# A hybrid decoder trunk: the first layer's input read features-first, ten idle products ahead, and the last sum and its transfers divided anew

## The chip, the cores and the metric

The kernel runs on one core of a Trainium2 chip. Its engines are TensorE (PE: products; PEld: the loading of their stationary operand, which overlaps), VectorE (DVE), ScalarE (ACT), GpSimd (POOL, unused here but for four constants) and SyncE (SP), which issues most of the transfers. Each engine works off its own queue in order. The metric is the device time of one execution in microseconds, taken as the median of several runs.

## What is computed

Two layers of a decoder trunk over 256 tokens of 2048 features, all float32. Each layer normalises x, multiplies it by one wide matrix, runs three mixers on parts of the result, gates and merges them, and adds the projection back to x. At the end there is one more normalisation.

```python
def rms_norm(x, w):
    y = xf * lax.rsqrt(jnp.mean(xf * xf, axis=-1, keepdims=True) + EPS)
    return (y * w.astype(jnp.float32)).astype(x.dtype)

def hybrid_layer(x, norm_w, w_in, ...):
    h = rms_norm(x, norm_w)
    proj = h @ w_in                      # 2048 x 18064
    (qa, ka, va, za, qi, ki, wi, ub, zb, qc, kc, vc, zc, gates) = jnp.split(...)
    ...                                  # sparse attention, conformer conv, stick-breaking attention
    merged = g[:, :, 0] * y_a + g[:, :, 1] * y_b + g[:, :, 2] * y_c
    return x + merged @ w_out

def reference(x, ...):
    for i in range(DEPTH):               # 2
        x = hybrid_layer(x, ...)
    return rms_norm(x, final_norm_w)
```

## The kernel before, in words

Every float32 product is made from two halves. A matrix of weights arrives in `raw` by a transfer from SP (`load_unit`, 512 KB: two chunks of 128 inputs by 512 outputs, or four by 256), ScalarE casts it to the rounded type (`wh`, line 204), VectorE subtracts to get the low part (`wl`, line 208), and TensorE adds up wh × x_high, wh × x_low and wl × x_high (line 218 records all of these). `raw` has four buffers, `wh` and `wl` three each, so ScalarE's cast of one unit waits until TensorE has done with the unit three before. Transfers are asked for one after the other on SP's queue, each held behind the transfer kept in `first` at the beginning.

What matters here is the beginning of a layer and the end of the last one.

The beginning. Two column blocks of the wide matrix (512 columns of `O_UG`, then 512 of `O_UA`) are multiplied by x before x is normalised, in `chunk_first`: 16 chunks of 128 features in eight units of two chunks, 24 products of 256 tokens a unit. In layer 0 the first unit is loaded as two halves of 256 KB. The normalisation's factor is worked out meanwhile, and the results are scaled by it afterwards (`rb`, a row broadcast over the partitions). For this, x is needed with features on the partitions. x lies tokens-first in memory, so in layer 0 `start_0` has each quarter of x turned by TensorE (`x_turn`, line 373, eight transposes for four chunks), multiplied by the norm weights on the way out of PSUM by VectorE (line 383, in the first unit ScalarE too, line 382), rounded by ScalarE (line 385) and its low part taken by VectorE (line 386). ScalarE squares the tokens-first x (line 366) and sums along the row with its accumulator; `rsqrt_mean` makes the factor, `diag_cols` a diagonal matrix of it (line 307), and `spread` multiplies ones by that matrix (line 422) between the two chunks to get `rb` (line 423). While the second chunk runs, `follow` scales x by rb (`scale_x`, line 411), rounds it (line 412) and takes low parts (line 417), two chunks of features a unit. From then on the layer uses these `hx`.

In both chunks of layer 0's start the order on VectorE is the program's, and in the first chunk that of ScalarE and TensorE too (`manual_schedule`); elsewhere a scheduler orders by priority.

The constants (identity, ones, norm weights, masks, rotary tables, convolution weights) are one DRAM array; the first 288 columns come first of all (line 63), the other 1696 after the ninth load (line 199).

The end. In layer 1 the output projection is done in blocks of 512, 512, 512, 256 and 256 columns. The last 256 columns are done for 128 tokens at a time (48 products each). After each of these two, the block is added to x (line 889), squared and summed by ScalarE (line 894) into the fifth of five partial sums, multiplied by the final norm weight (line 895); then VectorE adds the five sums (line 391), `rsqrt_mean` makes the factor (lines 291 to 296), and four quarters of 512 columns are scaled, two by VectorE (line 936) and two by ScalarE (line 934), each followed by its transfer on SP's queue (line 937).

Of the kernel before, what the change touches and what calls it, by code (L numbers as in the profile page):

```python
# [8 lines left out]
F32 = mybir.dt.float32  # L9
# [33 lines left out]
C_ID, C_ONE, C_NW, C_CB, C_SM, C_UP, C_MEAN, C_COS, C_SIN, C_PR = (  # L43
    0, 128, 256, 288, 544, 672, 800, 928, 1184, 1440)
# [4 lines left out]
def trunk(ctx: ExitStack, tc: tile.TileContext, x, w_in, w_a, w_b, w_c, w_out,  # L49
# [12 lines left out]
    with tc.high_priority(offset=URGENT):  # L62
        first = [nc.sync.dma_start(cst[:, :C_CB], consts[:, :C_CB])]

    xcs = []

    def load_x(j, cols=((0, 512),)):
        for a, b in cols:
            if a == 0:
                xcs.append(tp.tile([P, NT, 512], F32, tag="t4", bufs=4, name=f"x0_{j}"))  # L70
            with tc.high_priority(offset=URGENT), tc.issue_after(first[0].ins):
                first[0] = nc.sync.dma_start(xcs[j][:, :, a:b], xin[:, :, j * 512 + a:j * 512 + b])

    load_x(0, ((0, 256),))
# [106 lines left out]
    def load_unit(w, k0, kn, segs, dst=None):  # L181
# [5 lines left out]
        with tc.high_priority():  # L187
            o = 0
            for c0, c in segs:
                with tc.issue_after(first[0].ins):  # L190
                    dma = nc.sync.dma_start(
                        raw[:, :, o:o + c],
                        w[k0 * P:(k0 + kn) * P, c0:c0 + c].rearrange("(k p) c -> p k c", p=P))
                o += c
            if count[0] <= 5:
                first[0] = dma
            if count[0] == 9:
                with tc.issue_after(dma.ins):
                    first[0] = nc.sync.dma_start(cst[:, C_CB:], consts[:, C_CB:])
# [53 lines left out]
    def chunk_first(act, units):  # L253
        acc = acc_tile()
        for k0 in range(0, KD, 2):
            ks, between = units(k0)
            for n, (j, i) in enumerate(((0, 0), (0, 1), (1, 0))):
                if n == 1 and between:
                    between()
                for k, w_ in ks:  # L260
                    for f in range(4):
                        mm = mult(acc[:, f // 2, (f % 2) * S:(f % 2) * S + S], w_[j][:, f * P:(f + 1) * P],
                                  part(act, i, k)[:, 0, :], k == 0 and n == 0 and f % 2 == 0,
                                  k == KD - 1 and n == 2)
            background(mm)
# [33 lines left out]
    def warm_sqrt():  # L299
        d = small(1, 2)  # L300
# [75 lines left out]
    def x_parts(ps, xn, k, nw, n=2, first=False):  # L376
        xT, ux = xn
        xs = xT[k // KC][:, k % KC:k % KC + n, :]
        i = k % 4
        if first:  # L380
            for j in range(n):
                nc.scalar.activation(hi(ux, k + j), ps[:, i + j:i + j + 1, :], AF.Copy, scale=nw[:, k + j:k + j + 1])  # L382
        nc.vector.tensor_mul(xs, ps[:, i:i + n, :], nw[:, k:k + n].unsqueeze(2).to_broadcast([P, n, S]))
# [11 lines left out]
    warm_sqrt()  # L395
    xn = (big(), parts(KD))
    ssq = small(8).rearrange("p (t j) -> p t j", t=NT)
    tail = None
    for layer in range(DEPTH):
        w = w_in[layer]  # L400
        nw = cst[:, C_NW + layer * KD:C_NW + (layer + 1) * KD]
# [5 lines left out]
        with tc.manual_schedule(engines={nc.vector.engine}), ExitStack() as order:  # L407
            def scale_x(i):
                k = i * 2
                xs = xT[k // KC][:, k % KC:k % KC + 2, :]  # L410
                nc.vector.tensor_mul(xs, xs, heads(rb, 2))
# [15 lines left out]
            def follow(k0):  # L427
                u = k0 // 2
                if u == 0:
                    spread(state["dg"])  # L430
                else:
# [12 lines left out]
                return advance_units(k0)  # L444
# [28 lines left out]
            def step(ps, k):  # L473
                high(loaded[0])
                rest = x_parts(ps, xn, k, nw)
                low(loaded[0])
                ready.append(loaded.pop(0))
                rest()
# [509 lines left out]
```

## Time and profile before

| | us |
|---|---|
| median of 3 runs | 2072.56 (2072.18 to 2073.11) |
| the profiled execution | 2072.41 |
| its span, first to last instruction | 2070.6 |
| TensorE busy | 2056.9 |
| VectorE busy | 1490.4 |
| ScalarE busy | 1067.4 |
| DMA, mean rate over the span | 190 GB/s |

The page of the profile gives busy times over the span; the chain of waits follows the work that ended last back to its releasers; a timeline lists instructions as start, duration, engine, line, operation, output and inputs, shape and count, and in brackets how long the engine had been idle and what ended that. Rows of a timeline are merged where an engine repeats itself. A windows row gives a stretch, its length, the busy time and number of instructions of PE, PEld, DVE, ACT and POOL, the granted clock, the share of the DMA engines' time and their rate. All times are from the start of the span.

### The profile page before, as it was taken

The page shows a single profiled execution, that of the slowest core. Times are in us where ns is not written, and L with a number is a line of the kernel's source. Part 1 is how long each engine was busy: PE and PEld are TensorE (multiplying, and loading weights), DVE is VectorE, ACT ScalarE, POOL GpSimd, SP SyncE. Part 2 cuts the span into 40 slices and gives each one's busy share as a digit, 9 for nine tenths or more (in the row PEclk, how much of TensorE's full clock was granted, in tenths as well). Part 3 has the DMA queues.
Part 4 walks back from the last instruction along what each step waited for, and adds up shares of the span by engine and source line. Part 5 has one row for each costly group of instructions (what it writes and reads, how often), then busy time and mean ns, then how long its engine had stood idle before and what let it go on. Part 6 is the DMA issues. An engine that isn't in the chain of part 4 may idle for free.

```text
span 2070.6 us, 28574 instructions
## 1 busy us (share of the span) xinstructions
PE 2056.9 (99%) x11056; PEld 1793.6 (87%) x11056; DVE 1490.4 (72%) x2037; ACT 1067.4 (52%) x1309; POOL 0.2 (0%) x4
## 2 busy tenths in 40 slices
PE   9999999999999999999999999999999999999998
PEld 8899888888888888888899998888888888888887
DVE  7678998688776856555576799976887757565555
ACT  6465555466444544444454655554664445444443
POOL 0000000000000000000000000000000000000000
PEclk9999999999999999999999999999999999999999
DMA  7677575665666666666666774756656667666664
GB/s 247 194 220 214 145 204 157 182 179 165 180 190 189 217 209 192 187 190 194 206 191 194 224 204 145 203 152 187 182 162 183 190 194 223 193 192 190 206 196 145
DMA packets 290984, 394.27 MB, mean 190 GB/s; under 512 B 16544, under 2 KB 181536, under 8 KB 290720
## 3 DMA queue, kind: packets, MB, share of 16 engines
q1 hardware_dynamic: 289760, 390.35, 63.6%
q8 instruction: 86, 1.41, 0.3%
q10 hardware_dynamic: 1088, 2.10, 0.3%
q14 instruction: 50, 0.41, 0.1%
HBM read 388.20 MB, written 4.19 MB: 190 GB/s over the span
## 4 chain that ended last, share of the span: by engine, by line
PE 99%; DMA 0%; DVE 0%; ACT 0%; issue 0%; ACTq 0%; SPq 0%
PE acc L218 95%; PE mm L653 1%; PE mm L684 1%; PE mm L373 0%; PE mm L709 0%; PE mm L824 0%; PE mm L772 0%; PE mm L736 0%; PE mm L701 0%; PE mm L758 0%; PE mm L624 0%; PE mm L739 0%; PE mm L774 0%; DMA x<-in_x_dram 0%; PE mm L760 0%; PE mm L763 0%
## 5 line engine op out<-in xcount | busy, mean ns | idle before, releaser
L208 DVE TENSOR_TENSOR wl<-raw,wh 128x1024 fp32r<-128x1024 f32 (+2 forms) x729 | 880.1, 1210 | 474.7 <-ACT wh L204 472.1
L204 ACT CAST wh<-raw 128x1024 fp32r<-128x1024 f32 (+2 forms) x728 | 757.5, 1042 | 848.1 <-PE acc L218 666.5
L218 PE MATMUL acc<-wh,s 128*128 128x512 f32 (+2 forms) x3200 | 775.5, 384 | 0.0
L218 PEld LDWEIGHTS acc<-wh,s 128*128 128x128 f32 x3200 | 587.0, 188 | 114.7
L218 PE MATMUL acc<-s,wh 128*128 128x512 f32 (+2 forms) x2912 | 645.1, 365 | 0.6 <-ACT s L382 0.6
L218 PEld LDWEIGHTS acc<-s,wh 128*128 128x128 f32 x2912 | 492.6, 190 | 62.7 <-ACT s L382 1.0
L218 PE MATMUL acc<-wl,s 128*128 128x512 f32 (+2 forms) x1600 | 417.4, 383 | 0.0
L218 PEld LDWEIGHTS acc<-s,wl 128*128 128x128 f32 x2656 | 356.6, 191 | 18.4
L218 PE MATMUL acc<-s,wl 128*128 128x256 f32 (+1 forms) x2656 | 365.1, 280 | 0.0
L218 PEld LDWEIGHTS acc<-wl,s 128*128 128x128 f32 x1600 | 295.6, 188 | 58.8
L359 DVE SCALAR_TENSOR_TENSOR s<-yT,cst,s 128x256 f32<-128x256 f32 x480 | 217.5, 478 | 0.4
L244 DVE TENSOR_TENSOR ev<-acc,ev 128x512 f32<-128x512 f32 (+2 forms) x60 | 38.4, 640 | 0.0
L857 DVE TENSOR_TENSOR ev<-acc,ev 128x512 f32<-128x512 f32 x32 | 22.0, 688 | 19.3 <-PE acc L218 19.3
L311 ACT CAST s<-ev 128x512 fp32r<-128x512 f32 (+1 forms) x40 | 21.3, 533 | 26.3 <-DVE ev L332 24.5
L325 DVE TENSOR_TENSOR ev<-ev,cst 128x384 f32<-128x384 f32 (+2 forms) x28 | 16.7, 595 | 23.9 <-ACT ev L323 23.8
L243 ACT COPY ev<-acc 128x512 f32<-128x512 f32 (+2 forms) x60 | 32.8, 546 | 0.4 <-PE acc L218 0.4
L312 DVE TENSOR_TENSOR s<-ev,s 128x512 fp32r<-128x512 f32 (+1 forms) x40 | 23.2, 581 | 6.8 <-ACT s L311 6.6
L322 ACT COPY ev<-ev 64x384 f32<-64x384 f32 (+2 forms) x28 | 15.2, 542 | 24.7 <-DVE ev L244 24.3
L849 ACT ACTIVATE ev<-acc 128x512 f32<-128x512 f32 x48 | 26.6, 591 | 0.1
L889 DVE TENSOR_TENSOR t<-acc,t 128x512 f32<-128x512 f32 (+1 forms) x18 | 10.6, 628 | 17.2 <-PE acc L218 17.2
L858 DVE TENSOR_TENSOR s<-s,ev 128x512 f32<-128x512 f32 x32 | 21.9, 685 | 0.0
L341 ACT ACTIVATE ev<-ev 128x512 f32<-128x512 f32 x28 | 17.6, 627 | 0.0
(173 smaller groups left out, 806.4 us busy)
## 6 DMA issues: line engine op xcount, KB each, us to landing
raw<-in_w_in_dram SPq DMA_DIRECT2D x555, 512.0 KB, 3.6
raw<-in_w_out_dram SPq DMA_DIRECT2D x64, 512.0 KB, 4.2
raw<-in_w_a_dram SPq DMA_DIRECT2D x32, 512.0 KB, 3.9
raw<-in_w_c_dram SPq DMA_DIRECT2D x32, 512.0 KB, 3.9
raw<-in_w_b_dram SPq DMA_DIRECT2D x32, 512.0 KB, 3.8
raw<-in_w_in_dram SPq DMA_DIRECT2D x18, 256.0 KB, 3.1
t<-in_x_dram SPq DMA_DIRECT2D x4, 512.0 KB, 6.0
x<-t ACTq DMA_DIRECT2D x4, 512.0 KB, 3.6
```

The lines of the kernel that those rows point to most:

```text
L204: nc.scalar.copy(u[1], u[0])
L208: sub = nc.vector.tensor_sub(u[2], u[0], u[1].bitcast(F32))
L218: newest[0] = nc.tensor.matmul(o, lhsT, rhs, start=start, stop=stop, skip_group_check=True)
L243: nc.scalar.copy(dst, acc[:, :, nt:])
L244: nc.vector.tensor_add(dst, acc[:, :, :nt], dst)
L311: nc.scalar.copy(h, src)
L312: nc.vector.tensor_sub(l, src, h.bitcast(F32))
L359: nc.vector.scalar_tensor_tensor(o, yT[:, c, q:q + S], wq, o, op0=ALU.mult, op1=ALU.add)
L653: nc.tensor.matmul(ps[:, q * S:(q + 1) * S], qi[i][:, hd, :], ki[j][:, 0, :], start=n == 0, stop=n == 2)
L849: nc.scalar.activation(sg[t], g[t], AF.Sigmoid)
L857: nc.vector.tensor_mul(sg[t], y[t], sg[t])
L858: nc.vector.tensor_add(dst, dst, sg[t])
```

## The change

A second copy of x is given as an input, `xt`: one row per partition, first the norm weights of both layers (32 columns), then for each of the 16 chunks of features the 256 tokens. Layer 0 reads this instead of the tokens-first x at its start; the residual still reads `x`.

- `x0n` holds the norm weights and chunk 0 (one transfer of 288 columns, first on SP's queue); chunk 1 follows alone, then pairs of chunks straight into `xn`. All 32 transposes of layer 0's start are gone.
- The first two loads of weights are issued by ScalarE's queue. The constants' first transfer is gone, and after the ninth load all 1984 columns come at once.
- TensorE begins with ten products of a 128x128 tile of zeros.
- `x_high` and `x_low` make the rounded and the low part straight from x, times the norm weight, one chunk at a time: two operations of 128x256 for each of ScalarE and VectorE instead of one of 128x512 (VectorE: instead of two).
- The squares are of the features-first x (`x_square`, ScalarE). VectorE adds them up over the chunks, and two products with a column of ones (`total_square`) sum over the partitions. They stand in the last unit of the first chunk, eight products in; `spread` stands eight products into the second chunk, in both layers.
- `scale_x` in layer 0 multiplies the plain x by norm weight and rb: two operations instead of one.
- In the first unit the order of products is hi, lo of the first chunk, then hi, lo of the second, then the weights' low parts.
- At the end four of the five partial sums are added beforehand (`known`, `half`), the square root takes the last one with the others as its bias, and one small operation fewer makes the factor. The scaling is divided into 256 columns (VectorE), 512 (ScalarE, with its own transfer), 640 and 640 (VectorE).

```diff
@@ start of the trunk
-    with tc.high_priority(offset=URGENT):
-        first = [nc.sync.dma_start(cst[:, :C_CB], consts[:, :C_CB])]
-    ...
-    load_x(0, ((0, 256),))
+    x0n = cp.tile([P, C_ID + S], F32, name="x0n")
+    idle = tp.tile([P, P], F32, tag="dg", bufs=1, name="idle")
+    nc.vector.memset(idle, 0.0)
@@ load_unit
+                if count[0] <= 2:
+                    nc.scalar.dma_start(raw[:, :, o:o + c], src)
+                else:
+                    with queued():
+                        dma = nc.sync.dma_start(raw[:, :, o:o + c], src)
+                    if count[0] <= 9:
+                        first[0] = dma
             if count[0] == 9:
-                    first[0] = nc.sync.dma_start(cst[:, C_CB:], consts[:, C_CB:])
+                    first[0] = nc.sync.dma_start(cst, consts)
@@ chunk_first
-            for n, (j, i) in enumerate(((0, 0), (0, 1), (1, 0))):
-                if n == 1 and between:
+            order = [(n, u) for n in range(3) for u in ks]
+            if between:
+                order = [(n, u) for u in ks for n in range(2)] + [(2, u) for u in ks]
+            for m, (n, (k, w_)) in enumerate(order):
+                if m == len(ks) and between:
                     between()
@@ x_parts (layer 1)
-        nc.vector.tensor_mul(xs, ps[:, i:i + n, :], nw[:, k:k + n]...)
-        if not first:
-            nc.scalar.copy(hi(ux, k, n), xs)
-        return lambda: nc.vector.tensor_sub(lo(ux, k, n), xs, hi(ux, k, n).bitcast(F32))
+        nc.vector.tensor_mul(xs, ps, nw[:, k:k + n]...)
+        split_at(ux, k, n, xs)
@@ loads of x
+    def load_x(k, n=2):
+        with tc.high_priority(offset=URGENT), queued():
+            first[0] = nc.sync.dma_start(xn[0][k // KC][:, k % KC:k % KC + n, :], xt[...])
+    with tc.high_priority(offset=URGENT), queued():
+        first[0] = nc.sync.dma_start(x0n, xt[:, :C_ID + S])
+    load_x(1, 1)
@@ scale_x
+                if layer:
                     nc.vector.tensor_mul(xs, xs, heads(rb, 2))
+                else:
+                    for j in range(2):
+                        nc.vector.scalar_tensor_tensor(xs[:, j, :], x_at(k + j), nw[:, k + j:k + j + 1], rb,
+                                                       op0=ALU.mult, op1=ALU.mult)
@@ follow
-                if u == 0:
-                    spread(state["dg"])
...
-                return advance_units(k0)
+                return advance_units(k0)[0], None if u else lambda: spread(state["dg"])
@@ layer 0's first chunk
+            def x_high(k):
+                for j in range(k, k + 2):
+                    nc.scalar.activation(hi(ux, j)[:, 0, :], x_at(j), AF.Copy, scale=nw[:, j:j + 1])
+            def x_low(k):
+                for j in range(k, k + 2):
+                    nc.vector.scalar_tensor_tensor(lo(ux, j)[:, 0, :], x_at(j), nw[:, j:j + 1],
+                                                   hi(ux, j)[:, 0, :].bitcast(F32), op0=ALU.mult, op1=ALU.subtract)
+            def x_square(k):
...
+                    nc.scalar.activation(new.rearrange("p (k t) -> p k t", t=S), xs, AF.Square)
...
+                if k >= 4:
+                    nc.vector.tensor_add(sq, sq, new)
+            def step(k):
+                x_high(k)
                 high(loaded[0])
+                x_low(k)
                 low(loaded[0])
                 ready.append(loaded.pop(0))
+                for q in {4: (0,), 6: (2, 4), 8: (6,), 10: (8,), 12: (10, 12), 14: (14,)}.get(k, ()):
+                    x_square(q)
+            def total_square():
+                ps = mm_tile()
+                for t in range(NT):
+                    nc.tensor.matmul(ps[:, t:t + 1], state["sum"][:, t * P:(t + 1) * P], ones[:, :1], ...)
+                state["dg"] = diag_cols(rsqrt_mean(ps[:, :NT], D))
             def start_0(k0):
                 if k0 == 0:
                     load(2)
+                    warm_sqrt()
+                    load_x(2)
+                    load()
+                    load_x(4)
+                    load()
+                    ps = mm_tile()
+                    for _ in range(10):
+                        nc.tensor.matmul(ps[:, :P], idle, idle, start=True, stop=True)
...
+                if k0 < 14:
+                    step(k0 + 2)
+                    if k0 < 10:
+                        load_x(k0 + 6)
                     load()
+                    return next_unit(k0), None
+                sq = state["sq"]
+                state["sum"] = state["sq2"][:, :S]
+                nc.vector.tensor_add(sq[:, :2 * S], sq[:, :2 * S], sq[:, 2 * S:])
+                nc.vector.tensor_add(state["sum"], sq[:, :S], sq[:, S:2 * S])
+                return advance_units(k0)[0], total_square
@@ the end
+        known, half = small(2), small(2)
+            nc.vector.reduce_sum(known, ssq[:, :, :4], axis=AX.X)
+            nc.vector.tensor_scalar(half, known, -0.5 / D, -0.5 * EPS, op0=ALU.mult, op1=ALU.add)
+            nc.vector.tensor_scalar(known, known, 1.0 / D, EPS, op0=ALU.mult, op1=ALU.add)
...
-            r = rsqrt_mean(ssq_total(ssq[:, t:t + 1, :]), D)
-            for j in range(4):
-                js = slice(j * 512, (j + 1) * 512)
+                nc.scalar.activation(r, ss, AF.Sqrt, scale=1.0 / D, bias=known[:, t:t + 1])
+                nc.vector.tensor_scalar(m, ss, -0.5 / D, half[:, t:t + 1], op0=ALU.mult, op1=ALU.add)
+                nc.vector.reciprocal(r, r)
+                nc.vector.tensor_scalar(b, r, r, m, op0=ALU.mult, op1=ALU.mult)
+                nc.vector.scalar_tensor_tensor(r, b, 1.5, r, op0=ALU.add, op1=ALU.mult)
+                for j0, j1, eng in ((0, 256, nc.sync), (1536, D, nc.scalar), (256, 896, nc.sync), (896, 1536, nc.sync)):
...
-                    nc.sync.dma_start(out[t * P:(t + 1) * P, js], xfr[t][:, js])
+                    eng.dma_start(out[t * P:(t + 1) * P, js], xfr[t][:, js])
```

In the built program the order on VectorE around the sum of squares is: the addition of the last squares, the cast of `upper_r` (which reads the constants), the halving addition, the cast of `ones_r`, the last addition; then the low part of the second chunk's first weights, and behind it the factor's small operations.

More of the change, by code (lines that the diff above doesn't have):

```diff
@@ L400, in trunk @@
         w = w_in[layer]
-        nw = cst[:, C_NW + layer * KD:C_NW + (layer + 1) * KD]
+        nw = (cst if layer else x0n)[:, C_NW + layer * KD:C_NW + (layer + 1) * KD]
         pr = cst[:, C_PR + layer * P_END:C_PR + (layer + 1) * P_END]
@@ L485, in start_0 @@
                     nc.vector.tensor_copy(loaded[0][1], loaded[0][0])
-                    rest = x_parts(state[0], xn, 0, nw, first=True)
+                    x_high(0)
                     high(loaded[1])
-                    rest()
-                    for u in loaded:
+                    x_low(0)
+                    for u in loaded[:2]:
                         low(u)
-                    ready.extend(loaded)
-                    loaded.clear()
-                    load_x(0, ((256, 512),))
```

125 lines of the change are left out of this document (55 added, 70 removed).

## The prediction

> **What bounds the kernel now.** I read the page's head first, then the chain of waits, then the two places where that chain is not a product.
>
> ```profile
> span 2070.6 us, 28574 instructions
> PE 2056.9 (99%) x11056; PEld 1793.6 (87%) x11056; DVE 1490.4 (72%) x2037; ACT 1067.4 (52%) x1309; POOL 0.2 (0%) x4
> ```
>
> TensorE is idle for 2070.6 − 2056.9 = 13.7 us in all. The chain of waits over the first 40 us shows where the front part lies:
>
> ```profile
> 1.16 2.96 DMA x<-in_x_dram
> ...
> 4.26 1.10 PE mm L373 x4
> ...
> 5.38 0.85 ACT s L382 x2
> ...
> 8.33 1.09 PE mm L373 x4
> ...
> 11.90 0.87 PE mm L373 x8
> ...
> 34.64 0.43 PE mm L422 x2
> ```
>
> The chain runs DMA, transposes (L373), ScalarE, and from 9.42 on it stays on TensorE; transposes take 1.09 + 3 × 0.87 = 3.7 us between products. The timeline gives the products' speed:
>
> ```profile
> 5.91 2.09 PE L218 MATMUL acc<-s,wh 128*128 128x256 f32 x8 [0.56 <-ACT s L382]
> ...
> 9.07 1.88 PE L218 MATMUL acc<-s,wh 128*128 128x256 f32 x8
> ...
> 10.79 1.11 PE L218 MATMUL acc<-s,wl 128*128 128x256 f32 x8
> ```
>
> ```profile
> 52.18 2.08 PE L218 MATMUL acc<-s,wh 128*128 128x256 f32 x16
> ...
> 55.06 2.08 PE L218 MATMUL acc<-s,wh 128*128 128x256 f32 x16
> ...
> 56.98 1.12 PE L218 MATMUL acc<-s,wl 128*128 128x256 f32 x8
> ...
> 57.94 2.00 PE L218 MATMUL acc<-s,wh 128*128 128x512 f32 x8
> ```
>
> Eight products take 1.88 us at 9.07 and 1.11 at 10.79, so the array runs at half speed until about 10.7. A unit (two input chunks, 24 products) takes 55.06 − 52.18 = 2.88 us, 0.12 each. The first two products' chunks last from 5.91 to 57.94, 52.0 us; 16 units are 46.1, and the rest is transposes, half speed, short waits and one spread (L422, 0.43). After 57.94 nothing of the change slows or relieves TensorE until the end: in layer 1 the spread only moves by eight products, its input being ready at both places. So 57.94 and the last product (2062.04, ahead of the addition at 2062.06 shown with the tail) are the two marks.
>
> **The head.** Removed from TensorE: 32 transposes. Added: ten f32 products of zeros, two one-column products, none of them long. An f32 product of 256 columns is two records and 0.43 us at full speed (L422); of 128 columns half of that, and at half speed 0.43 again.
>
> ```profile
> 0.80 0.06 DVE L76 MEMSET eps<- 128x1 f32 x1 [0.80 <-PEq L977]
> ...
> 4.83 0.43 DVE L485 CAST wh<-raw 128x512 fp32r<-128x512 f32 x1 [1.69 <-DMA raw<-in_w_in_dram]
> 5.38 0.84 ACT L382 ACTIVATE s<-mm,cst 128x256 fp32r<-128x256 f32 x2 [3.16 <-PE mm L373]
> ...
> 9.51 1.04 ACT L204 CAST wh<-raw 128x1024 fp32r<-128x1024 f32 x1 [2.78 <-DMA raw<-in_w_in_dram]
> ```
>
> The zeros are written first on VectorE, so the ten run from about 0.95 to 0.95 + 10 × 0.43 = 5.3. By then x's first chunk and the first weights (which now leave on ScalarE's queue at the start, not third on SP's) have landed and been cast: raw was there at 4.83 as third transfer, so at 3.9 to 4.3 (an estimate), plus a cast of 0.43. ScalarE's two issues (SP's take 0.46, the row at 19.39 below) and its table load are over by 3.2. First product at 5.3, against 5.91.
>
> What decides is the third load of weights (chunks 2 and 3): the cast at 9.51 began when it landed. Ahead of it and with it go 1.59 MB (x 0.15 + 0.13 + 0.26, weights 0.26 + 0.26 + 0.52), against 1.72 before.
>
> ```profile
> 5.00:7.00 2.00, 1.44 (x7) 1.09 (x6) 0.97 (x3) 1.34 (x3) 0.00 (x0) 1.00 0.86 225
> 7.00:17.50 10.50, 10.17 (x75) 9.91 (x75) 8.40 (x12) 4.71 (x6) 0.00 (x0) 1.00 1.02 379
> ```
>
> The last columns are DMA share and GB/s. 0.13 MB at 379 GB/s is 0.3 us; the slow stretch from 5 to 7 us, where x's second 256 columns (1 KB rows) were due, costs up to 2 × (379 − 225) / 379 = 0.8 us and mostly goes, since only two small transfers keep short rows. So it lands between 8.0 and 9.2; I take 8.6. Cast 1.04, first product of that unit at 9.7. The 24 products before it end at 5.3 + 24 × 0.12 = 8.2 at full speed, so there is a wait here of 1.5 us, which also hides half-speed products.
>
> In sentences of its own: the Trainium skill (DMA: Bandwidth & Descriptors, Issuing engines are not separate DMA queues) says that transfers issued by different engines interleave on the same 16 engines and only issue time is saved, which speaks against moving weights to ScalarE's queue. The share of 0.86 to 1.02 in the rows above agrees; by that rule alone the third load would land at the upper end, 9.2, and the sum below would be 0.6 longer.
>
> From 9.7 on TensorE needs 15 units × 2.88 = 43.2, the spread 0.43, the one-column products 0.05: next mark 53.4, unless its feeders are slower. Their prices:
>
> ```profile
> 18.38 0.63 ACT L366 ACTIVATE ev<-x 128x512 f32<-128x512 f32 x1
> ...
> 41.41 1.28 DVE L438 TENSOR_TENSOR ev<-acc,rb 128x512 f32<-128x512 f32 x2
> ```
>
> ```profile
> 51.43 2.35 DVE L208 TENSOR_TENSOR wl<-raw,wh 128x1024 fp32r<-128x1024 f32 x2
> ...
> 71.19 0.87 DVE L359 SCALAR_TENSOR_TENSOR s<-yT,cst,s 128x256 f32<-128x256 f32 x2
> ```
>
> ScalarE per unit: two scaled copies 0.84, cast 1.04, square 0.63 = 2.5, under 2.88. VectorE per unit: weights' low part 1.13 (2.35 − 1.22 in a full queue), two low parts of x 0.78 to 0.87, one addition of squares 0.60 to 0.69: 2.5 to 2.8. Both fit, with little to spare. Now the sum of squares: TensorE stands on it eight products into unit 8, at 9.7 + 6 × 2.88 + 0.96 = 27.9. ScalarE, from 9.7, has six pairs of copies (5.0), six casts (6.2) and the squares (0.84 + 7 × 0.63 = 5.25): the last square at 26.2. Behind it on VectorE stand an addition (0.6), the cast of upper_r (0.2), the halving addition (0.6), the cast of ones_r (0.2) and the last one over 256 columns (0.4): 2.0, so 28.2, a stall of 0.3. With full queues and overlap VectorE's own list (17.6 us from 9.7) gives 27.3, no stall; with every duration in full (7 × 1.22 + 6 × 0.96 + 6 × 0.69 + 1.6 = 20.0) it gives 29.7, a stall of 1.8. I take 0.3. Then the diagonal: VectorE first does one low part of weights (1.2), five small operations of 0.2 and two of 0.25, so 28.2 + 2.8 = 31.0; TensorE arrives 24 products later, 28.3 + 2.88 = 31.2. Nothing, or 0.5 if it slips.
>
> In the second chunk the scaling by rb becomes two operations (0.87 for 0.69) and rb comes a product group (0.96) later: VectorE is 8 × 0.18 + 0.96 = 2.4 us later at the end. The cover: its last low part ended at 51.43 + 2.35 = 53.8 and was first used at 56.98, two thirds into the unit of 55.06; 3.2 us. Enough; without that cover it would cost up to 0.8. The squares' old ScalarE work and its read of the accumulator were off the path.
>
> Mark: 53.4 + 0.3 = 53.7 against 57.94, a gain of 4.2 (1.6 with the worst of all these, 5.1 with a landing at 8.0 and no stall).
>
> **The tail.**
>
> ```profile
> 2062.06 0.42 DVE L889 TENSOR_TENSOR t<-acc,t 128x256 f32<-128x256 f32 x1 [2.57 <-PE acc L218]
> ...
> 2063.06 0.16 DVE L391 TENSOR_REDUCE sm<-sm 128x1 f32<-128x5 f32 x1
> 2063.25 0.29 ACT L291 ACTIVATE sm<-sm,eps 128x1 f32<-128x1 f32 x1 [0.22 <-DVE sm L391]
> ...
> 2063.78 0.16 DVE L294 TENSOR_TENSOR sm<-sm 128x1 f32<-128x1 f32 x1
> 2063.97 0.16 DVE L295 SCALAR_TENSOR_TENSOR sm<-sm 128x1 f32<-128x1 f32 x1
> ...
> 2064.36 0.72 ACT L934 ACTIVATE s<-s,sm 128x512 f32<-128x512 f32 x1 [0.81 <-DVE sm L296]
> 2064.36 0.88 DVE L936 TENSOR_SCALAR s<-s,sm 128x512 f32<-128x512 f32 x2
> 2064.88 0.33 SPq L937 DMA_DIRECT2D out_dram<-s  x1
> ```
>
> The reduction (2063.06 to 2063.25) and one small operation (0.2) leave the path: 0.4. The other sums over known columns are VectorE's, under the last 16 + 80 products. The first transfer waits for 256 columns instead of 512, 0.24 instead of 0.44.
>
> ```profile
> 2065.50:2065.75 0.25, 0.00 (x0) 0.00 (x0) 0.00 (x0) 0.19 (x1) 0.00 (x0) 0.50 0.15 57
> ...
> 2065.50:2069.00 3.50, 0.00 (x0) 0.00 (x0) 0.00 (x0) 0.19 (x1) 0.00 (x0) 0.50 0.90 300
> 2069.00:2070.60 1.60, 0.00 (x0) 0.00 (x0) 0.00 (x0) 0.00 (x0) 0.00 (x0) 0.50 0.00 0
> ```
>
> Data flow 0.8 us after the first issue and fill the engines till 2068.95, 4.6 after the scale is known at 2064.36; the last 1.6 us stay. New, counted from the scale: the first 0.13 MB flows from 1.05 to about 1.45, ScalarE's 512 columns from 0.72 + 0.8 = 1.5, then 0.92 MB at about 350 GB/s, to 4.2. Gain 0.4 + 0.4, of which I take 0.75 (0.4 if the engines gain nothing, 1.0 at best).
>
> **Sum.** The profiled execution took 2072.41 (span 2070.6, 1.8 around it, unchanged), 0.15 under the median of the runs. 2072.4 − 4.2 − 0.75 = 2067.4.
>
> **The rivals.** (1) The clock stays at half speed to 10.7 or 14 us, as if the ten products of zeros did nothing for it. For: before, half speed lasted 6.4 us from the first transpose. Against: ten products keep TensorE busy from 0.95 without a gap. Price: 24 products at 0.235 end at 10.9 instead of the start at 9.7, 1.2 us, and another 1.4 if one more unit is slow: 2068.6 to 2070.0. In sentences of its own: the Trainium skill (TensorE: Matmul & The Clock Gate, Part 1: The HAM clock gate) says that full speed comes after a busy window of about 3.4 us whose start is not tied to the kernel; counted from 0.95 that is 4.4 to 7.8, inside the wait that I have, so by it the sum stays. This trace fits it loosely (half speed to 10.7).
>
> (2) VectorE becomes the bound: stall 1.8 at the sum of squares and 0.5 at the spread instead of 0.3: 2069.4. For: 2.5 to 2.8 of 2.88 us. Against: overlap in every full queue of the trace.
>
> (3) Slower than before, by the constants. Now one transfer of 1.0 MB brings the identity, the ones and upper_r, and VectorE stands on upper_r ahead of the last two additions, TensorE behind them.
>
> ```profile
> 19.39 0.46 SPq L199 DMA_DIRECT2D cst<-in_consts_dram  x1
> ...
> 28.61 0.22 DVE L547 CAST upper_r<-cst 128x128 fp32r<-128x128 f32 x1
> ...
> 30.08 0.48 DVE L307 TENSOR_SCALAR dg<-cst,sm 128x128 f32<-128x128 f32 x2
> ```
>
> It was issued at 19.39 and its first reader ran at 28.6 without a wait. It costs from a landing at 27.3 on, one for one, and makes the kernel slower than before from 27.3 + 5.0 = 32.3; a landing at 37 gives 2077. Against: issued around 16, with 0.5 MB of weights ahead, it needs 1.5 MB, 4 us at 379 GB/s.
>
> (4) The third load lands at 8.0 or before and nothing stalls: 2066.3.
>
> **How the numbers follow.** Forecast 0.58 (its own range 2066.6 to 2068.6), (1) 0.15, (2) 0.11, (3) 0.05, (4) 0.11. Faster by over 0.2% (which is what a measurement of this kernel can tell from no change) is below 2068.4: (4) and nearly all of the forecast, and a start of the others: 0.70. Slower 0.06, same 0.24. Range: 2065.8 to 2070.3 leaves out the slow rival and the far end of (1).
>
> **What would show it.** No L373 in layer 0; first real product near 5.3 and at 0.12; a wait of TensorE of 1 to 2 us before the unit of chunks 2 and 3, ended by ScalarE's cast behind a DMA; at most 0.5 us of wait at the one-column products; the first 128x512 products near 53.7; the scale known 2.0 us after the last product (before 2.3). I am wrong if the wait before that unit is longer than 3 us, if VectorE ends a wait of more than a microsecond, or if the constants do.

## The result, and the profile after

Twelve executions of the changed kernel have a median of 2067.81 us (2067.51 to 2068.87), twelve of the kernel before 2072.91 us (2071.65 to 2074.53). The ratio is 0.9976, with a 95% interval of 0.9968 to 0.9984: 5.1 us faster. The profiled execution took 2067.92 us, 4.49 less than the one of before.

The head of the page of the changed kernel:

```profile
span 2066.1 us, 28588 instructions
PE 2057.2 (100%) x11048; PEld 1793.8 (87%) x11048; DVE 1493.0 (72%) x2054; ACT 1066.7 (52%) x1307; POOL 0.2 (0%) x4
```

TensorE's idle time is now 2066.1 − 2057.2 = 8.9 us instead of 13.7. Of these, 7.85 are the tail and 1.05 the start. The chain of waits of the changed kernel up to 62 us (start, duration, what):

```profile
0.82 0.17 DVE idle L69
...
1.05 4.63 PE mm L533 x20
5.68 21.98 PE acc L215 x176
27.66 0.03 issue
27.70 0.61 PE mm L520 x4
28.30 2.98 PE acc L215 x24
31.28 0.43 PE mm L428 x2
```

The DMA, the transposes and ScalarE are gone from it; from the zeros' memset on it is TensorE alone. "100%" does not mean that it works at its pace, though, as the timeline of TensorE in the changed kernel shows:

```profile
5.33 3.01 PE L215 MATMUL acc<-s,wh 128*128 128x256 f32 x16
8.18 1.12 PE L215 MATMUL acc<-s,wl 128*128 128x256 f32 x8
9.17 2.18 PE L215 MATMUL acc<-s,wh 128*128 128x256 f32 x16
```

Sixteen products take 8.18 − 5.33 = 2.85 us where 1.92 is full speed: (2.85 − 1.92) / 0.115 = 8 of them ran at half speed, until about 7.2 (0.115 is what a product of 256 columns takes longer at half speed, 0.235 for 0.12). Then the third load of weights and the first 512-wide product, from the timeline of the changed kernel:

```profile
8.07 1.05 ACT L201 CAST wh<-raw 128x1024 fp32r<-128x1024 f32 x1 [1.12 <-DMA raw<-in_w_in_dram]
```

```profile
53.62 2.00 PE L215 MATMUL acc<-s,wh 128*128 128x512 f32 x8
```

Mark 1 stands at 53.62 (57.94 before), 4.32 earlier. Most of this, 3.36, is there already at the first product of chunks 2 and 3: 9.17 now, and in the timeline of the kernel before

```profile
12.53 2.16 PE L218 MATMUL acc<-s,wh 128*128 128x256 f32 x16
```

The other 0.96 are the two groups of transposes behind that place (0.87 each), less about 0.75 that the new sum of squares costs: TensorE waits 0.23 for VectorE's last addition, as the row of its weight loads shows, and then spends 0.46 on the 128x1 products.

```profile
27.69 0.52 PEld L520 LDWEIGHTS mm<-cst,t 128*128 128x128 f32 x4 [0.23 <-DVE t L558]
```

The tail, on the timeline of the changed kernel:

```profile
2058.27 0.42 DVE L925 TENSOR_TENSOR t<-acc,t 128x256 f32<-128x256 f32 x1 [2.44 <-PE acc L215]
...
2060.30 0.72 ACT L981 ACTIVATE s<-s,sm 128x512 f32<-128x512 f32 x1 [0.73 <-DVE sm L977]
2060.30 1.28 DVE L983 TENSOR_SCALAR s<-s,sm 128x256 f32<-128x256 f32 x3
```

From the last addition's start to the scale it is 2.03 us (2.30 before), to the span's end 7.83 (8.54 before): 0.71 gained. But from mark 1 to that addition it is 2058.27 − 53.62 = 2004.65, where it was 2062.06 − 57.94 = 2004.12. The changed kernel loses 0.53 us in a stretch that the change does not touch.

### The profile page after: what moved, and what is told of

Its sections match the earlier page's. It is cut to its first block, busy times and chain, and to the rows that moved or that the text cites. A ratio compares the mean times of both kernels' runs of the same rounds, so it can differ in the third digit from the quotient of the medians.

```text
span 2066.1 us, 28588 instructions
## 1 busy us (share of the span) xinstructions
PE 2057.2 (100%) x11048; PEld 1793.8 (87%) x11048; DVE 1493.0 (72%) x2054; ACT 1066.7 (52%) x1307; POOL 0.2 (0%) x4
## 4 chain that ended last, share of the span: by engine, by line
PE 100%; DVE 0%; ACT 0%; DVEq 0%; issue 0%
PE acc L215 95%; PE mm L689 1%; PE mm L720 1%; PE mm L745 0%; PE mm L860 0%; PE mm L808 0%; PE mm L772 0%; PE mm L737 0%; PE mm L533 0%; PE mm L373 0%; PE mm L794 0%; PE mm L660 0%; PE mm L775 0%; PE mm L810 0%; PE mm L799 0%; PE mm L796 0%
```

## The experiments

Times below are medians of ten or eleven executions (of the last kernel there is one execution); "mark 1" is the first 128x512 product in the profiled execution. Kernels of one group ran on one chip against the same runs of the kernel before: 2072.45 us in the first group, 2072.64 in the second, 2072.41 in the third. The interval of each ratio is about ±0.0009 (1.9 us), wider than most steps here, so the marks in the traces decide and the medians support them.

### First group

**Without the zeros.**

```diff
-                    ps = mm_tile()
-                    for _ in range(10):
-                        nc.tensor.matmul(ps[:, :P], idle, idle, start=True, stop=True)
```

> The changed kernel without its ten products of zeros. Theory (the ten make the array fast early): the first real product runs at about 4.6, when the first weights' cast (4.15 + 0.43) is done, but half speed lasts about 6.4 us from it, as in the kernel before (4.26 to 10.7), so to about 11; 24 products at 0.235 end near 10.2 instead of 9.1, and three or four more of the next unit are slow (0.4); the stall of 0.23 at the sum of squares goes: first 128x512 product at 54.8 to 55.1 (changed kernel 53.62), time 2069.0 to 2069.3. Rival (the zeros do nothing for the speed, the landing of the third load of weights sets the unit of chunks 2 and 3): that unit still starts at 9.2, first 128x512 product at 53.6, time 2067.8.

Measured: 2067.99 us, ratio 0.9978 (0.9969 to 0.9987), mark 1 at 54.08. TensorE's timeline without the zeros:

```profile
4.84 3.75 PE L215 MATMUL acc<-s,wh 128*128 128x256 f32 x16 [4.84 <-DVE wh L531]
8.39 1.80 PE L215 MATMUL acc<-s,wl 128*128 128x256 f32 x8
10.04 2.06 PE L215 MATMUL acc<-s,wh 128*128 128x256 f32 x16
...
28.26 0.50 PE L520 MATMUL mm<-cst,t 128*128 128x1 f32 x4
28.62 1.20 PE L215 MATMUL acc<-s,wh 128*128 128x256 f32 x8
```

The first 24 products run at half speed nearly to their end, and the next unit starts at 10.04 instead of 9.17. Of these 0.87 us, 0.41 come back: 0.20 because no product waits at the sum any more, 0.10 because the 128x1 products then take 28.62 − 28.26 = 0.36 instead of 0.46, and 0.11 in the unit of chunks 2 and 3 itself. So half speed ended here after about 5 us, not 6.4, and the zeros are worth 0.46 in this pair of executions, a third of what I expected. The medians, 2067.99 against 2067.81 and 2067.67, are of different groups and cannot confirm it.

**Zeros in the kernel before** (seven of them, ahead of its first transposes; the memset as in the change).

> The kernel before with seven products of zeros ahead of its first transposes, nothing else changed. Theory (the zeros shorten half speed wherever the other inputs are there): full speed from about 7.3 instead of 10.7, the eight products at 9.07 take 1.11 instead of 1.88 and start 0.3 earlier, the unit of chunks 2 and 3 starts near 11.6 instead of 12.53; first 128x512 product 57.0 to 57.4 (before 57.94), time 0.5 to 0.9 us under the kernel before. Rival (in that kernel the transfers and the transposes behind them set the pace, so speed alone buys nothing): 57.9, no change.

Measured: 2071.96 us, ratio 0.9995 (0.9986 to 1.0004), mark 1 at 57.14. The mark is 0.8 earlier, as the theory has it. But the kernel with the new tail alone, whose head is that of the kernel before and has no zeros, has its mark at 57.12 (below): so this run proves nothing about zeros. The two marks without zeros, 57.94 and 57.12, show that the head of the kernel before varies by 0.8 us from execution to execution.

**The sum of squares by one product.**

```diff
-                    nc.tensor.matmul(ps[:, t:t + 1], state["sum"][:, t * P:(t + 1) * P], ones[:, :1], start=True, stop=True)
-                state["dg"] = diag_cols(rsqrt_mean(ps[:, :NT], D))
+                nc.tensor.matmul(ps[:, :S], ones, state["sum"], start=True, stop=True)
...
+                nc.vector.reciprocal(r, r)
...
+                nc.vector.scalar_tensor_tensor(rb, a, 1.5, r, op0=ALU.add, op1=ALU.mult)
```

> The changed kernel with the sum of squares formed by one product of the ones (128x128) and the 256 summed columns, issued after 16 products of that unit instead of 8, so that every partition has the sum at once; the 128x1 products, the diagonal and the spread go, and the inverse root is worked out over 256 columns by VectorE. Theory (the changed kernel pays 0.23 of stall, 0.46 of 128x1 products and 0.43 of spread there): only 0.43 stays, first 128x512 product at 52.9 to 53.0 instead of 53.62, time 2067.1. Rival (VectorE has nothing to spare, and five operations over 256 columns of about 0.4 instead of five of 0.16 and two of 0.25 make it late): a wait of TensorE ended by VectorE in the second chunk, first 128x512 product at 53.6 or later.

Measured: 2068.33 us, ratio 0.9979 (0.9971 to 0.9988). The scheduler moved three 512-wide products ahead of mark 1, so it is read one group later: 54.69 against 55.46, a gain of 0.77. At 72 us only 0.24 of it is left. Why, the timelines of VectorE and of the weight loads in this kernel show:

```profile
29.79 1.74 DVE L525 RECIPROCAL t<-t 128x256 f32<-128x256 f32 x1
31.57 0.43 DVE L526 TENSOR_TENSOR t<-t 128x256 f32<-128x256 f32 x1
```

```profile
49.34 1.02 PEld L215 LDWEIGHTS acc<-s,wl 128*128 128x128 f32 x8 [0.21 <-DVE wl L205]
...
59.51 1.70 PEld L215 LDWEIGHTS acc<-s,wh 128*128 128x128 f32 x8 [0.41 <-ACT wh L201]
...
61.97 0.76 PEld L215 LDWEIGHTS acc<-s,wh 128*128 128x128 f32 x4 [0.18 <-DVE s L424]
```

The reciprocal over 256 columns takes 1.74 us, four times the 0.4 that I had put for each operation. The price could have been read beforehand: the kernel before has such a reciprocal at 699.5 us (line 293), and it takes 1.74 there too. VectorE is then behind in the second chunk, and TensorE waits three times. The rival's mechanism holds; only its place is later than either theory said.

**The tail alone**, in the kernel before. The diff is that of the tail in the change, with the one-column buffer of the first square root that it brings.

> The kernel before with the changed kernel's last sum and output transfers alone. Theory (the tail's gain stands by itself): first 128x512 product unchanged at 57.9, scale known 2.03 us after the last product instead of 2.30, from the last product to the span's end 7.85 instead of 8.56, time 0.7 us under the kernel before (ratio 0.9997). Rival (the division of the transfers buys nothing, only the shorter sum does): 8.3, 0.3 us.

Measured: 2072.44 us, ratio 1.0000 (0.9991 to 1.0008). The scale is known 2.04 us after the last addition's start (2063.76 − 2061.72) and the span's end comes 7.88 after it: the tail itself gains its 0.66. Yet mark 1 at 57.12 and the addition at 2061.72 are 2004.60 apart. From the timelines, first this kernel, then the one with seven zeros and the old tail:

```profile
57.12 2.00 PE L218 MATMUL acc<-s,wh 128*128 128x512 f32 x8
...
2061.72 0.42 DVE L889 TENSOR_TENSOR t<-acc,t 128x256 f32<-128x256 f32 x1 [2.44 <-PE acc L218]
```

```profile
57.14 2.00 PE L220 MATMUL acc<-s,wh 128*128 128x512 f32 x8
...
2061.26 0.42 DVE L894 TENSOR_TENSOR t<-acc,t 128x256 f32<-128x256 f32 x1 [2.57 <-PE acc L220]
```

With the old tail this stretch takes 2004.12 (with the seven zeros and in the kernel before), with the new one 2004.60 to 2004.67 (in this kernel, in two executions of the changed kernel and in the eight others of this study that have it and whose mark can be compared). So the loss of 0.5 us comes with the tail's edit. Set against the kernel before, more than half of it, 0.27, lies at eight places, four in each layer (475 to 529 us and 1501 to 1555 us of the kernel before), where eight 512-wide products in a row each time take 0.034 longer. One of them, in the kernel before and then in this one:

```profile
1501.49 1.98 PE L218 MATMUL acc<-wh,s 128*128 128x512 f32 x8
```

```profile
1500.98 2.01 PE L218 MATMUL acc<-wh,s 128*128 128x512 f32 x8
```

No product stands in another order there. The changed kernel has the same steps at the same products, and the kernel with seven zeros and the old tail has none of them, so this is not a variation between executions. What makes them was not found; that the tail's edit also changes which small buffers exist, and could so have moved others, was not tested. The tail's gain net of it is about 0.2.

### Second group

**The changed kernel again**, unaltered.

> The changed kernel unaltered, to stand in one comparison with the next three and to see how far its head varies from run to run. Theory (the moment of full speed varies between executions, and the ten products bring it before the third load's cast ends at 9.1, so that this kernel does not feel it): first real product 5.3, full speed at 7 to 8, unit of chunks 2 and 3 at 9.1 to 9.2, first 128x512 product at 53.5 to 53.7, time 2067.8. Rival (the variation reaches this kernel too): that unit at 9.5 or later, first 128x512 product 54.0 or later.

Measured: 2067.67 us (2067.31 to 2068.41), ratio 0.9978 (0.9969 to 0.9986), mark 1 at 53.46. TensorE's timeline in this execution:

```profile
1.05 4.54 PE L533 MATMUL mm<-idle 128*128 128x128 f32 x20 [1.05 <-DVE eps L71]
5.33 2.17 PE L215 MATMUL acc<-s,wh 128*128 128x256 f32 x16
7.34 1.12 PE L215 MATMUL acc<-s,wl 128*128 128x256 f32 x8
9.00 2.17 PE L215 MATMUL acc<-s,wh 128*128 128x256 f32 x16 [0.54 <-ACT wh L201]
```

Full speed came at about 5.5 here, against 7.2 in the first profile, in the same code, and before the 7 to 8 that I expected. The 24 products end 0.8 us sooner, and TensorE spends it waiting for the third load's cast (landed at 7.90). This is the wait that the prediction had, in a third of its length; mark 1 moves by only 0.16. Two kernels below (late constants, no additions) have the same order of transfers and products up to here, and wait 1.23 and 1.17 us at this place, with the load cast at 8.26 and 8.15. So the forecast wait does appear in full when full speed comes early enough.

**The transposes' time given back.**

```diff
+            def turn(n):
+                ps = mm_tile()
+                for _ in range(n):
+                    nc.tensor.matmul(ps[:, :P], idle, idle, start=True, stop=True)
...
+                if k0 in (2, 4, 8):
+                    turn(4)
...
+                        turn(2)
                         step(2)
```

> The changed kernel with fourteen more f32 products of zeros (128x128 each, two records of 0.107) at the places where the kernel before had 28 of its 32 transposes (two ahead of the ninth product, four ahead of each of the units of chunks 2 and 3, 4 and 5, 8 and 9): as much of TensorE's time as those 28, 3.0 us, but nothing waits for them. Theory (TensorE's own time sets the head, and the transposes' removal is the main gain): two of them and some of the next four lie in front of the unit of chunks 2 and 3, the rest adds one for one, less the 0.23 of stall at the sum of squares: first 128x512 product at 56.2 to 56.5 (changed kernel 53.62), time 2070.5. Rival (the gain comes from x arriving in its final layout, so that ScalarE and VectorE are earlier, and TensorE has slack): first 128x512 product below 55.

Measured: 2070.17 us (2069.12 to 2070.50), ratio 0.9987 (0.9978 to 0.9996), 2.5 us over the changed kernel. The profiled execution is the fastest of its eleven, with mark 1 at 54.79. Its head on TensorE's timeline:

```profile
1.05 3.88 PE L540 MATMUL mm<-idle 128*128 128x128 f32 x20 [1.05 <-DVE eps L71]
4.68 1.19 PE L215 MATMUL acc<-s,wh 128*128 128x256 f32 x8
...
8.07 1.05 PE L526 MATMUL mm<-idle 128*128 128x128 f32 x8
8.88 2.16 PE L215 MATMUL acc<-s,wh 128*128 128x256 f32 x16
```

Full speed came at about 4 (the same twenty records took 3.88 instead of 4.63). So the first six of the fourteen fit into time in which TensorE would have waited for the third load, and that unit starts at 8.88; the other eight cost 1.6, less the wait at the sum. My expectation had counted the six as well, so by its mark (below 55) this execution is the rival's, while the median is near the theory's 2070.5. In executions with full speed later the six probably cost too, which would explain the 2.5 of the median; none of those has a trace. So 1.2 to 2.5 us of the gain is TensorE time that the transposes took, the smaller figure where TensorE would have waited for the load anyway.

**The first weights back on SP's queue.**

```diff
-                if count[0] <= 2:
-                    nc.scalar.dma_start(raw[:, :, o:o + c], src)
```

> The changed kernel with the first two loads of weights back on SP's queue, behind x's first two chunks; all of SP's later issues move back by two (0.9 us). Theory (the transfers share the same bandwidth, at 310 to 390 GB/s from 1.75 us on, so only the order changes): first product at 5.5 to 5.9 instead of 5.33, third load of weights lands at 8.1 to 8.4 instead of 8.05, first 128x512 product at 53.6 to 53.8, time within 0.2 us of the changed kernel. Rival (issue time on SP's queue sets the landing): third load lands at 9.0, its unit starts at 10.1 instead of 9.17, first 128x512 product at 54.3, time 0.7 us longer.

Measured: 2068.67 us, ratio 0.9983 (0.9974 to 0.9991), 1.0 us over the changed kernel; mark 1 at 54.37. The waits in its timeline:

```profile
8.84 1.04 ACT L198 CAST wh<-raw 128x1024 fp32r<-128x1024 f32 x1 [1.19 <-DMA raw<-in_w_in_dram]
...
9.94 2.17 PE L212 MATMUL acc<-s,wh 128*128 128x256 f32 x16 [1.11 <-ACT wh L198]
```

The third load is cast from 8.84 on. In the eight profiles of this study with the changed kernel's order of transfers this cast begins between 7.74 and 8.26, so it is 0.6 to 1.1 later here, about the 0.94 by which the issue moved (3.05 against 2.11). The theory falls, and the rival's numbers hold: this landing follows the issue time on the queue. The DMA engines also moved somewhat less (301 and 329 GB/s from 4 to 6 and 6 to 8 us, against 317 and 367), so the issue time need not be all of it.

**The 128x1 products eight later** (after 16 products of their unit instead of 8, nothing else).

> The changed kernel with the 128x1 products issued after 16 products of their unit instead of 8; nothing else. Theory (TensorE stands 0.23 us on VectorE's last addition and then has slack at the spread): the stall goes, the diagonal is ready at about 30.4 for a spread at 31.1, first 128x512 product at 53.4, time 0.2 us under the changed kernel. Rival (the diagonal becomes late): a wait of TensorE at the spread ended by VectorE, first 128x512 product at 53.6 or later.

Measured: 2067.46 us (2067.03 to 2067.92), ratio 0.9976 (0.9967 to 0.9985), mark 1 at 53.28. TensorE's timeline and VectorE's at that place:

```profile
26.50 2.08 PE L215 MATMUL acc<-s,wh 128*128 128x256 f32 x16
28.42 0.50 PE L521 MATMUL mm<-cst,t 128*128 128x1 f32 x4
28.79 1.20 PE L215 MATMUL acc<-s,wl 128*128 128x256 f32 x8
```

```profile
30.11 0.48 DVE L308 TENSOR_SCALAR dg<-cst,sm 128x128 f32<-128x128 f32 x2
```

No wait at the sum, none at the spread (the diagonal is done at 30.59, the spread runs at 30.90). From the unit of chunks 2 and 3 to mark 1 it takes 44.15 us instead of 44.45, and the median is 0.2 under that of the changed kernel. It has the lowest median here, though by less than the runs can tell apart.

### Third group

**Third load on ScalarE's queue too** (the late sum, and `count[0] <= 3`).

> The changed kernel with the 128x1 products after 16 products of their unit instead of 8 (as before in this study) and, new, the third load of weights issued on ScalarE's queue behind the first two (at about 1.6 instead of 2.11; SP's next issues move up by one, 0.47). Theory (issue time sets the landing of the third load, and its cast sets the unit of chunks 2 and 3 whenever full speed comes early): landing at 7.4 to 7.6 instead of 7.9 to 8.05, the unit at 8.5 to 8.7 instead of 9.0, first 128x512 product at 52.8 to 53.0, time 2067.0 to 2067.2; in an execution with late full speed the 24 products before it end at 9.1 and nothing is gained. Rival (ScalarE starts x's first copies later behind its third issue and its table load, or the bandwidth is full): unit at 9.0 or later, first 128x512 product at 53.3, as with the late sum alone.

Measured: 2067.88 us, ratio 0.9979 (0.9970 to 0.9988), mark 1 at 54.23. The timeline of DMA issues and of the cast behind the third load:

```profile
1.17 1.37 SPq L394 DMA_DIRECT2D s<-in_xt_dram  x3
...
1.72 0.40 ACTq L187 DMA_DIRECT2D raw<-in_w_in_dram  x1
...
2.59 0.43 SPq L190 DMA_DIRECT2D raw<-in_w_in_dram  x1
...
8.95 1.04 ACT L201 CAST wh<-raw 128x1024 fp32r<-128x1024 f32 x1 [0.72 <-DMA raw<-in_w_in_dram]
...
10.04 1.22 PE L215 MATMUL acc<-s,wh 128*128 128x256 f32 x8 [1.77 <-ACT wh L201]
```

Issued 0.4 earlier, the load was cast 0.7 to 1.2 later than in the eight profiles above (the cast began when ScalarE's wait for this load ended): three transfers of x and the fourth load now leave SP at the same time. Here the DMA engines moved more, 365 and 389 GB/s in the same two stretches, which fits transfers that share the engines with this load. The move that gained for two loads loses for the third.

**The same without the zeros.**

> The kernel above without its ten products of zeros. Theory (full speed comes 3 to 6.4 us after TensorE's first product, at a moment that varies between executions; without the zeros that first product is at 4.7, so half speed lasts to between 7.7 and 11.1): first 128x512 product between 53.0 and 54.9, by the moment in this execution, median of the runs 0.5 to 1.0 us longer than the kernel above. Rival (full speed is not brought forward by the zeros): the same time within 0.2 us.

Measured: 2068.11 us, ratio 0.9979 (0.9970 to 0.9988), 0.2 over the kernel with them; mark 1 at 53.75, ahead of it. Its third load was cast at 8.49 (late again, if less so), and full speed came about 3.5 us after its first product at 4.70. Neither theory is borne out; 0.2 us cannot be told apart. With the first run without zeros this leaves the zeros' worth open: one pair of marks speaks for them, the other against, though in the second pair the landing differs too (8.95 and 8.49).

**The constants two loads later.**

> The changed kernel with the constants' one transfer issued after the eleventh load of weights instead of the ninth: at about 20 instead of 15.30, since the loads ahead of it wait for free buffers. Theory (first needed at 26.4 to 27.5; it lands some 8 us after its issue, as the profile of the changed kernel shows): landing at 28 to 29, TensorE waits 1 to 2 us for it at the 128x1 products, first 128x512 product at 54.3 to 55.5. Rival (the landing takes 4 to 5 us with less queued ahead, so two loads' delay is still covered): no wait, first 128x512 product at 53.5 to 53.7.

Measured: 2067.55 us, ratio 0.9977 (0.9968 to 0.9986), mark 1 at 53.51. Two rows of its timeline, and its row in the table of DMA issues (size, and us from issue to landing):

```profile
20.81 0.46 SPq L196 DMA_DIRECT2D cst<-in_consts_dram  x1
...
28.29 0.50 PE L520 MATMUL mm<-cst,t 128*128 128x1 f32 x4
```

```profile
cst<-in_consts_dram SPq DMA_DIRECT2D x1, 992.0 KB, 6.3
```

Issued 5.5 us later, the constants landed 6.3 us after their issue, at 27.1, and hold nobody up. That is between theory (8) and rival (4 to 5), and just short of the 27.3 from which the prediction had them cost. The scheduler also moved the 128x1 products and the casts of constants behind five more products, which makes this a weak test of the price, though a clear one of the cover.

**Without the additions of squares** (one execution).

> The changed kernel without VectorE's six additions of the squares of chunks 4 to 15 (so its sum of squares holds four chunks only); 4.1 us of VectorE's work. Theory (VectorE keeps up with TensorE and is only 0.23 late at the sum): that stall goes, nothing else moves, first 128x512 product at 53.3 to 53.4. Rival (VectorE is the bound of the head): the units before the sum get shorter too, first 128x512 product at 53.0 or earlier.

Measured: mark 1 at 53.41, 2067.70 us. TensorE's timeline at the sum:

```profile
27.59 0.50 PE L518 MATMUL mm<-cst,t 128*128 128x1 f32 x4
27.95 1.20 PE L215 MATMUL acc<-s,wh 128*128 128x256 f32 x8
```

The wait goes, the units stay at 2.88 us. From the unit of chunks 2 and 3 to mark 1 it takes 44.16 us instead of 44.45. So with 4.1 us less work on VectorE TensorE is 0.3 faster, all of it at the sum: VectorE does not bound the rest of the head.

## Why the prediction was right

The time forecast was 2067.4, the median 2067.81, inside the range. Step by step:

- **First product** at 5.3: measured 5.33. The ten zeros end it, as worked out, at half speed throughout; where full speed came sooner it stands at 4.7 to 5.2.
- **Third load**: taken at 8.6 between 8.0 and 9.2; it landed at 8.05 and 7.90. The term was 0.6 too late. Its two written parts, 0.3 and 0.8, lead from 9.51 to 8.4 only; that the issue of the third load comes 0.9 earlier when two weights move to another queue was not in the sum, and the run with them put back shows that the landing moves by about as much. The sum by the rule of the Trainium skill (DMA: Bandwidth & Descriptors, Issuing engines are not separate DMA queues), which put the load at the upper end, does not hold here; that issue time is what a second engine saves does, at 0.6 to 1.1 us. The run with a third load on ScalarE's queue agrees with the rest of that rule, that transfers interleave.
- **The wait before that unit**, 1.5 us: none in the first profile, 0.54 in the second (1.2 in two kernels with the same head). The reason given, that the wait hides half-speed products, was right; in the first profile half speed took all of it. Unit start 9.17 and 9.00 instead of 9.7.
- **The sum of squares**: wait 0.23 for 0.3, but the 128x1 products cost 0.46 us of TensorE (27.70 to 28.16; 0.36 in the runs without a wait), not 0.05. I had priced them by their columns. Each of the two products comes with two loads of a 128x128 operand (the row of weight loads above, 0.52 us for the four); that these take the time is likely, but no run tests it apart.
- **The second chunk** without a wait of VectorE's, **no stall at the spread**: as forecast. Mark 1 53.7: measured 53.62 and 53.46. That the mark agrees to 0.1 is luck in part: the unit of chunks 2 and 3 starts 0.5 early, and the 128x1 products cost 0.4 more than I had put.
- **"After 57.94 nothing of the change slows or relieves TensorE until the end"** is the step that failed: 0.5 us, brought by the tail's edit, in steps whose cause is open.
- **Tail** 0.75: measured 0.71 in the tail itself, 0.27 by the shorter sum (0.4 forecast) and 0.44 by the transfers (0.4), and 0.2 net of that loss.
- **The constants** were to take 4 us from their issue around 16: issued at 15.30, they took 8.2. The price was half of what it had to be, and the cover held.

The sum by the trace is −4.32 + 0.53 − 0.71 = −4.50. The medians say −5.1 and −5.0; the profiled execution of the kernel before, 2072.41, lay up to 0.5 under the later medians of that kernel. With the same head the kernel with the new tail had mark 1 at 57.12, so the 4.32 belong to this pair of executions.

Of the rivals, (1) named the right unknown and a wrong price: without the zeros the unit starts 0.87 late and mark 1 0.46 in one execution, in the other the mark is early, and the zeros do not make full speed certain early. Its second price was also low: one more unit at half speed would be 24 × 0.115 = 2.8 us, not 1.4. By the Trainium skill (TensorE: Matmul & The Clock Gate, Part 1: The HAM clock gate) the busy window is about 3.4 us long and not tied to the kernel's start; by an estimate from that figure full speed would come 3.4 to 6.8 us after the first product, and the 3 to 6.4 measured (last section) agree roughly, the shortest lying under it. (2) falls by the run without the additions; (3) did not come about: the constants landed at 23.5, and in the run with late constants they held nobody up either, as far as that run goes; the early load of (4) is what happened, without the rest of it.

In rough shares, from runs that undo one part: the transposes 1.2 to 2.5 us, the two loads on ScalarE's queue 0.75 to 1.0, the zeros at most 0.5, the tail 0.2. They were not measured together, and need not add up: of the 5.1, between 0.9 (with the larger figures) and nearly 3 us stay without a run of their own, among them TensorE's waits of 0.56 and 0.33 in the first 9 us of the kernel before.

## What to carry to other kernels

Work out two times for the place where products first wait for data, the one by TensorE's pace and the one by the load, and change both: a faster start that ends in a wait buys nothing, and part of what is gained there is given back at the next wait (0.3 of 0.87 in the first run without zeros). Moving a load to another engine's queue paid here for the issues that the next load no longer stood behind, until more transfers left together. And price tiny f32 products, and an operation over 256 columns, by a row of that very operation, reciprocals above all: the kernel before may have one far from the place in question.

## What the runs showed of the hardware

**The moment of full speed varies from execution to execution.** Counted from TensorE's first product, it came after about 3 us (the run with the transposes' time), 4.4 and 6.2 (two executions of the changed kernel), 6.4 (the kernel before) and 5.0 (the kernel before with the new tail). The granted clock does not tell it: the window from 5 to 7 us of the kernel before says 1.00 at half speed. It has to be read from the spacing of products. The products of zeros count: in the run with the transposes' time full speed came at about 4, before the first real product at 4.68. The kernel before spread over 2.9 us in twelve executions and the changed one over 1.4. That this is the zeros' doing is not shown, and the changed kernel without them, with 0.9 us in eleven executions, speaks against it.

**An operation's price by columns is not one rate**: a reciprocal of 128x256 took 1.74 us, of 128x2 0.15; a multiplication of the same 256 columns 0.43.

**An edit can cost elsewhere.** The new tail lengthened 2004.12 us of unaltered order by 0.5 in every kernel that had it and can be compared, more than half of it in eight groups of eight 512-wide products.
